# Layer 1's input projection with 27 pairs of channel tiles: seven products of halves in place of eight

## The chip, the core and the metric

One NeuronCore of a Trainium2 chip runs the whole kernel; the other cores are idle. The metric is device time in microseconds (us), the median of three runs. Engines are named as in the profile: PE is the matmul array (PEld its weight loads), DVE, ACT and POOL are the vector, scalar and GpSimd engines, SP is the queue that issues most of the loads.

## What is computed

Two layers over 512 tokens of width 1024. Layer 0 mixes pooling and a stick-breaking attention; layer 1 is a gated short convolution. The change is in layer 1, whose mixer is

```python
proj = h @ w_in                       # h: 512 x 1024, w_in: 1024 x 8192
gb, gc, u, gate = jnp.split(proj, [D_CONV, 2 * D_CONV, 3 * D_CONV], axis=-1)
u = gc * u
conv = conv_b + sum(up[:, j:j + s] * conv_w[j] for j in range(CONV_WIDTH))   # up: u, padded by 2
y = gb * conv * jax.nn.silu(gate)
return y @ w_out                      # 2048 x 1024
```

and h is the normalised input, scaled and shifted by parameters that come from a conditioning vector c (`ada`, a 1024 x 3072 matrix for each layer). All data is float32.

## The kernel before

Activations lie transposed in SBUF: 128 channels on the partitions, 512 tokens in a row. Each float32 operand of a matmul is split into two float32r parts, hi (the value rounded by a cast on ACT) and lo (the value minus hi, on DVE); `hilo` does both. A product is then three matmuls, hi·hi, hi·lo and lo·hi (`mm3`, lines 189 to 193), with float32 sums in PSUM.

A weight tile ("unit") is 128 x 1024: 128 output channels, eight blocks of 128 for the contraction. `load_upto` issues its 512 KB load on SP into `raw` (3 buffers), `split_upto` makes `whi` and `wlo` (3 buffers each), `next_unit` keeps a few units ahead of use. `mtile` multiplies one unit with h: 8 x 3 matmuls of 128 x 128 weights against 512 tokens.

Layer 1 (`layer1`, lines 819 to 892): the units of the first channel tile are multiplied in two halves of 256 tokens, while h is still being made for the second half. Then, for each of 16 channel tiles j, `mtile` runs four times in the order gc, u, gate, gb; DVE and ACT form gc·u, the convolution (`acc`), the gate's SiLU and the products, and split the result into `yh` and `yl`. After j = 7 and after j = 15 an output projection of 8 units follows (`outproj`, `outproj_norm`), each of which adds its result into x (`x_add`, line 226). Between the channel tiles `ada_next(1)` loads 512 KB of the conditioning matrix and takes a dot product on DVE (line 114), one after each j until the list `ada_rest` is empty; layer 0's first output projection does two per unit.

PE and SP run in the order in which the code is written. The order on DVE, ACT and POOL is set by a scheduler that works out priorities from the program; on the chip every engine takes its instructions strictly in that order and waits on semaphores for the others.

## Time and profile before

| | |
|---|---|
| median of three runs | 896.88 us (896.63 to 898.55) |
| profiled execution, its time | 897.1 us |
| profiled execution, its span | 895.4 us |
| PE busy, share of the span | 98% |
| DVE, ACT, POOL busy | 64%, 39%, 6% |
| granted clock of PE, mean | 0.992 of full speed |
| data moved | 106.69 MB, mean 119 GB/s |

The profile is of one execution. Its span, from the first to the last recorded instruction, is 1.7 us shorter than the time that is measured around it. Matmuls overlap in their records (a record of 0.39 us starts 0.23 us after the one before), so the busy share of PE says that PE always has something in hand; how fast it goes is read from the starts of its records.

### The profile page before, as it was taken

The numbers are of one execution on the slowest core, as the hardware profiler recorded it, in microseconds if no ns is written. First come the engines' busy times: TensorE is split into PE (matmuls) and PEld (weight loads), VectorE is DVE, ScalarE is ACT, GpSimd is POOL, SyncE is SP. The second block draws the span as 40 slices with busy tenths as digits, with TensorE's granted clock in tenths as the row PEclk, the third lists the DMA queues.
The fourth block names the chain that finished last, engine by engine and source line by source line (L and its number), as shares of the span: only waits on it lengthen the run. The fifth ranks groups of instructions, "written<-read, shape, count | busy, mean of one in ns | idle before, by whom it ended". The sixth has DMA issues, their size and how long they took to land.

```text
span 895.4 us, 10797 instructions
## 1 busy us (share of the span) xinstructions
PE 877.2 (98%) x4172; PEld 733.9 (82%) x4172; DVE 573.8 (64%) x816; ACT 353.5 (39%) x552; POOL 56.4 (6%) x106
## 2 busy tenths in 40 slices
PE   8999999999999999999999999999999999999995
PEld 5788788888888888888998888888888888888884
DVE  6989979788877777695665555445334444444445
ACT  5366564655312655564442222222122222222331
POOL 1002301202000102010000000000000000000002
PEclk9999999999999999999999999999999999999997
DMA  8852132123876221123413333333322233222202
GB/s 308 298 177 73 53 100 89 60 71 118 305 279 238 85 81 59 59 79 107 145 48 118 118 121 126 128 120 119 94 94 94 98 102 106 95 94 94 94 25 94
DMA packets 30725, 106.69 MB, mean 119 GB/s; under 512 B 3409, under 2 KB 3537, under 8 KB 30674
## 3 DMA queue, kind: packets, MB, share of 16 engines
q1 hardware_dynamic: 30386, 105.48, 34.7%
q8 instruction: 33, 0.54, 0.3%
q10 hardware_dynamic: 288, 0.52, 0.2%
q14 instruction: 18, 0.15, 0.1%
HBM read 103.90 MB, written 2.10 MB: 118 GB/s over the span
## 4 chain that ended last, share of the span: by engine, by line
PE 90%; DVE 6%; ACT 1%; issue 1%; DMA 1%; SPq 0%; POOL 0%; DVEq 0%; ACTq 0%
PE m L191 25%; PE m L192 25%; PE m L193 25%; PE zb L662 2%; PE av L397 2%; PE m L664 2%; PE z L384 1%; DVE f L368 1%; PE zb L143 1%; PE z L353 1%; PE zb L806 1%; PE zb L805 1%; PE zb L807 1%; PE z L354 1%; PE zb L191 1%
## 5 line engine op out<-in xcount | busy, mean ns | idle before, releaser
L60 ACT CAST whi<-raw 128x1024 fp32r<-128x1024 f32 (+1 forms) x137 | 142.5, 1041 | 411.7 <-PE m L192 323.9
L191 PE MATMUL m<-hh,whi 128*128 128x512 f32 x768 | 300.5, 391 | 0.6 <-DVE yt L408 0.6
L193 PE MATMUL m<-hh,wlo 128*128 128x512 f32 x768 | 299.1, 389 | 0.0
L192 PE MATMUL m<-hl,whi 128*128 128x512 f32 x768 | 299.0, 389 | 0.0
L61 DVE TENSOR_TENSOR wlo<-raw,whi 128x1024 fp32r<-128x1024 f32 (+1 forms) x137 | 165.1, 1206 | 114.2 <-ACT whi L60 110.8
L193 PEld LDWEIGHTS m<-hh,wlo 128*128 128x128 f32 x768 | 144.1, 188 | 30.2
L191 PEld LDWEIGHTS m<-hh,whi 128*128 128x128 f32 x768 | 144.2, 188 | 30.1 <-DVE yt L408 0.8
L192 PEld LDWEIGHTS m<-hl,whi 128*128 128x128 f32 x768 | 144.3, 188 | 29.2
L191 PE MATMUL m<-yh,whi 128*128 128x512 f32 (+1 forms) x288 | 105.7, 367 | 0.0
L192 PE MATMUL m<-yl,whi 128*128 128x512 f32 (+1 forms) x288 | 105.3, 365 | 0.0
L193 PE MATMUL m<-yh,wlo 128*128 128x512 f32 (+1 forms) x288 | 105.2, 365 | 0.0
L226 DVE SCALAR_TENSOR_TENSOR x<-m,small,x 128x512 f32<-128x512 f32 (+1 forms) x36 | 24.8, 691 | 64.1 <-PE m L193 64.1
L191 PEld LDWEIGHTS m<-yh,whi 128*128 128x128 f32 x288 | 54.3, 189 | 8.9
L192 PEld LDWEIGHTS m<-yl,whi 128*128 128x128 f32 x288 | 54.3, 189 | 8.8
L193 PEld LDWEIGHTS m<-yh,wlo 128*128 128x128 f32 x288 | 54.3, 189 | 8.8
L362 POOL TENSOR_SCALAR_AFFINE_SELECT s<-s 128x128 f32<-128x128 f32 x64 | 43.2, 698 | 270.2 <-ACT s L357 252.4
L368 DVE TENSOR_TENSOR_SCAN f<-f,mask 128x512 f32<-128x512 f32 (+1 forms) x64 | 52.2, 844 | 0.0
L846 DVE TENSOR_TENSOR u<-m,t 128x512 f32<-128x512 f32 x16 | 11.1, 692 | 56.0 <-PE m L193 49.6
L60 ACT CAST yh<-t 128x512 fp32r<-128x512 f32 x40 | 24.9, 621 | 45.7 <-DVE t L441 20.3
L859 DVE TENSOR_TENSOR t<-t,m 128x512 f32<-128x512 f32 x15 | 10.3, 688 | 50.3 <-PE m L193 50.3
L114 DVE CUSTOM_DVE_ANT_0 araw<-araw,cbc,cst 128x1024 f32<-128x1024 f32 x32 | 40.5, 1277 | 2.0 <-DMA araw<-in_ada 2.0
L845 POOL MEMSET u<- 128x16 f32 x16 | 1.8, 112 | 423.3 <-DVE t L854 347.5
(180 smaller groups left out, 972.1 us busy)
## 6 DMA issues: line engine op xcount, KB each, us to landing
raw<-in_w1m SPq DMA_DIRECT2D x64, 512.0 KB, 3.3
raw<-in_w0m SPq DMA_DIRECT2D x36, 512.0 KB, 3.3
araw<-in_ada SPq DMA_DIRECT2D x32, 512.0 KB, 4.9
ring<-in_ada SPq DMA_DIRECT2D x16, 512.0 KB, 5.7
raw<-in_w0o SPq DMA_DIRECT2D x16, 512.0 KB, 4.2
raw<-in_w1o SPq DMA_DIRECT2D x16, 512.0 KB, 3.2
raw<-in_w0s SPq DMA_DIRECT2D x8, 512.0 KB, 5.8
x<-in_x SPq DMA_DIRECT2D x8, 256.0 KB, 4.7
```

Source lines behind the costliest of these rows:

```text
L60: a = self.nc.scalar.copy(out=hi, in_=src)
L61: b = (eng or self.nc.vector).tensor_tensor(out=lo, in0=src, in1=hi.bitcast(F32), op=ALU.subtract)
L114: ins = nc.vector.tensor_tensor_reduce(raw, raw, self.cbc, 1.0, self.cst[:, b : b + 1], ALU.mult, ALU.add, col)
L191: mm(ps, wh, xh, start=first, stop=False)
L192: mm(ps, wh, xl, start=False, stop=False)
L193: mm(ps, wl, xh, start=False, stop=last)
L226: self.nc.vector.scalar_tensor_tensor(x, ps[:, sl], self.adacol(layer, 2, mt), x, ALU.mult, ALU.add)
L362: nc.gpsimd.affine_select(out=sw[:, d], in_=sw[:, d], pattern=[[-1, P]], compare_op=ALU.is_gt, fill=0.0, base=0, channel_multiplier=1,)
L368: nc.vector.tensor_tensor_scan(r, r, self.mask[:, S - n :][:, ::-1], 1.0, ALU.mult, ALU.max)
L397: self.nc.tensor.matmul(ps[:, kb * P :], vs[:, kb, c : c + P], t[:, o : o + w], start=(n == 0 and kb == 0), stop=(n == 1 and kb == 3),)
L662: mm(pv[bank], h[:, tok[bank]], w[:, :512], start=f and n == 0, stop=l and n == 2)
L664: mm(pq[bank - 4], w[:, col[bank - 4]], h, start=f and n == 0, stop=l and n == 2)
```

## The change

Channel tiles j = 2 to 15 of layer 1 are taken in pairs of weight tiles: (gc, u) of each j and (gb, gate) of each j but the last, 27 pairs. The contraction of 1024 is cut into two halves of 512 and the tokens into two halves of 256. Of a pair, W11 and W12 are the two halves of the first tile, W21 and W22 of the second; B11 to B22 are the quarters of h (first digit the half of the contraction, second the half of the tokens). In place of eight products of such halves seven are formed, of W11, W12, W22 and four sums of weights (S1 to S4) against B11, B21, B22 and four sums of quarters of h (T1 to T4). A product is 4 x 3 matmuls of 128 x 128 weights against 256 tokens (`product`). Tiles j = 0 and 1, the gate and gb of j = 15, and both output projections stay as they were.

T1 to T4 are made once (`make_t`, on DVE and ACT) during tile j = 1, from a float32 copy of h (`hf`, one more ACT instruction for each piece of h). The sums of weights are made per pair: `load_pair` loads the second tile into `r2`, the first into `r1`, half of the second once more into `r3` (all on SP), and then POOL issues a transfer that reads 512 KB from DRAM and adds it into `r2` (W11 and W21, so that `r2` holds W11 + W21 and W21 + W22); S2 and S4 are two further additions on DVE. `r1` takes the three `raw` buffers in turn, `r2` two buffers, `r3` two. `prep` splits each of the seven weights; the six buffers of `whi` and `wlo` hold the results, and splitting runs five products ahead of PE. `step` moves sums out of PSUM between the products: three results are read out from one bank as they accumulate. The last two products of a pair stand between those of the next pair.

All 24 dot products for layer 1's conditioning are now done in layer 0's first output projection (`ada_next(3)` in place of `ada_next(2)`); layer 1 has none. The first operation of the convolution moves from DVE to ACT.

```diff
...
@@ -69,14 +69,14 @@
         return len(self.units) - 1
     def load_upto(self, n):
-        while self.loaded < min(n, len(self.units)):
+        while self.loaded < min(n, self.limit):
...
-                    self.outproj(0, ys, lambda mt: self.ada_next(2))
+                    self.outproj(0, ys, lambda mt: self.ada_next(3))
...
+    PAIRED = range(2, 16)
...
     def plan_l1(self):
         io = self.io
         self.l1_first = len(self.units)
-        for g in range(2):
-            for j in range(8 * g, 8 * g + 8):
-                for part in (1, 2, 3, 0):
-                    self.add_unit(io["w1m"][part * 16 + j])
-            for mt in range(8):
-                self.add_unit(io["w1o"][mt, g])
+        self.limit = self.l1_first + 8
+        for j in range(2):
+            for part in (1, 2, 3, 0):
+                self.add_unit(io["w1m"][part * 16 + j])
+        for mt in range(8):
+            self.add_unit(io["w1o"][mt, 0])
+        for part in (3, 0):
+            self.add_unit(io["w1m"][part * 16 + 15])
+        for mt in range(8):
+            self.add_unit(io["w1o"][mt, 1])
...
+    def make_t(self):
+        nc = self.nc
+        ha, hb = slice(0, 256), slice(256, S)
+        sub = dict(op=ALU.subtract)
+        self.T = {}
+        t12 = self.ap.tile([P, 4, 1024], F32R, tag="vs", name="t12")
+        sums = []
+        for k in range(4):
+            f1, f2 = self.hf[k], self.hf[k + 4]
+            a = self.yp.tile([P, S], F32, tag="yl", name="ta")
+            b = self.yp.tile([P, S], F32, tag="yl", name="tb")
+            nc.vector.tensor_tensor(out=a[:, ha], in0=f1[:, ha], in1=f1[:, hb], **sub)
+            nc.vector.scalar_tensor_tensor(a[:, hb], f2[:, hb], -1.0, a[:, ha], ALU.mult, ALU.subtract)
+            nc.vector.tensor_tensor(out=b[:, ha], in0=f2[:, hb], in1=f1[:, hb], **sub)
+            nc.vector.scalar_tensor_tensor(b[:, hb], a[:, hb], -1.0, f2[:, ha], ALU.mult, ALU.subtract)
+            sums.append((a, b))
+        for k in range(4):
+            a, b = sums[k]
+            d = t12[:, k]
+            self.hilo(d[:, :S], d[:, S:], a)
+            e = self.ap.tile([P, 1024], F32R, tag="sf"[k % 2], name="t34", bufs=2)
+            self.hilo(e[:, :S], e[:, S:], b)
+            for n, (t, o) in enumerate(((d, 0), (d, 256), (e, 0), (e, 256))):
+                self.T[n + 1, k] = (t[:, o : o + 256], t[:, S + o : S + o + 256])
...
+    def load_pair(self, m1, m2):
+        nc, w = self.nc, self.io["w1m"]
+        i = self.pair_no = getattr(self, "pair_no", -1) + 1
+        r1 = self.wp.tile([P, 1024], F32, tag="raw", name="r1", bufs=3)
+        r2 = self.ap.tile([P, 1280], F32, tag=("ah", "al")[i % 2], name="r2")[:, :1024]
+        r3 = self.ap.tile([P, S], F32, tag=("kle", "klo")[i % 2], name="r3")
+        nc.sync.dma_start(r2, w[m2])
+        nc.sync.dma_start(r1, w[m1])
+        nc.sync.dma_start(r3, w[m2, :, 512:])
+        nc.gpsimd.dma_start(
+            r2.rearrange("p (a c) -> p a c", a=2),
+            w[m1 : m2 + 1 : m2 - m1, :, :512].rearrange("a p c -> p a c"), accum_op=ALU.add,
+        )
+        return dict(r1=r1, r2=r2, r3=r3)
...
+    def prep(self, pr, what):
+        nc = self.nc
+        r1, r2 = pr["r1"], pr["r2"]
+        k1, k2 = slice(0, 512), slice(512, 1024)
+        src = {
+            "W11": r1[:, k1], "W12": r1[:, k2], "W22": pr["r3"], "S1": r2[:, k2], "S2": r2[:, k2],
+            "S3": r2[:, k1], "S4": r1[:, k2],
+        }[what]
+        if what == "S2":
+            nc.vector.tensor_tensor(out=src, in0=src, in1=r1[:, k1], op=ALU.add)
+        self.prod_no += 1
+        d = self.wp.tile([P, 1024], F32R, tag=("whi", "wlo")[self.prod_no % 2], name="wp", bufs=3)
+        self.hilo(d[:, k1], d[:, k2], src)
+        if what == "W12":
+            nc.vector.tensor_tensor(out=src, in0=src, in1=r2[:, k2], op=ALU.add)
+        pr[what + "d"] = d
...
+    def product(self, pr, what, mov, bank, first):
+        d = pr.pop(what + "d")
+        mm = self.nc.tensor.matmul
+        ps = pr[bank]
+        for k in range(4):
+            hi, lo = d[:, k * P : (k + 1) * P], d[:, 512 + k * P : 512 + (k + 1) * P]
+            bh, bl = self.moving(mov, k)
+            mm(ps, hi, bh, start=first and k == 0, stop=False, skip_group_check=True)
+            mm(ps, hi, bl, start=False, stop=False, skip_group_check=True)
+            mm(ps, lo, bh, start=False, stop=k == 3, skip_group_check=True)
...
+    def step(self, pr, n):
+        nc = self.nc
+        ha, hb = slice(0, 256), slice(256, S)
+        copy = nc.scalar.copy
+        if n == 1:
+            pr["X"] = self.zbank()[:, ha]
+            self.product(pr, "W11", "B11", "X", True)
+            pr["t12"] = self.t512("sgp")
+            copy(out=pr["t12"][:, ha], in_=pr["X"])
+        elif n == 5:
+            pr["Z"] = self.zbank()[:, ha]
+            self.product(pr, "S1", "T1", "Z", True)
+        elif n == 6:
+            self.product(pr, "S2", "T2", "X", False)
+            copy(out=pr["t12"][:, hb], in_=pr["X"])
+        elif n == 2:
+            pr["Y"] = self.mbank()[:, ha]
+            self.product(pr, "W12", "B21", "Y", True)
+            pr["o1"] = self.t512(pr["tag"])
+            nc.vector.tensor_tensor(out=pr["o1"][:, ha], in0=pr["Y"], in1=pr["t12"][:, ha], op=ALU.add)
+        elif n == 7:
+            self.product(pr, "S3", "T3", "X", False)
+            t3 = self.t512("u%d" % pr["odd"], S + PAD, 1)[:, ha]
+            copy(out=t3, in_=pr["X"])
+            pr["o2"] = self.t512(pr["tag"])
+            nc.vector.scalar_tensor_tensor(pr["o2"][:, hb], pr["Z"], -1.0, t3, ALU.mult, ALU.subtract)
+        elif n == 4:
+            self.product(pr, "W22", "T4", "X", False)
+            nc.scalar.activation(pr["o2"][:, ha], pr["X"], AF.Copy, scale=-1.0)
+        else:
+            self.product(pr, "S4", "B22", "Z", False)
+            nc.vector.tensor_tensor(out=pr["o1"][:, hb], in0=pr["Z"], in1=pr["t12"][:, hb], op=ALU.add)
+            pr["done"](pr["o1"], pr["o2"])
...
+        nc.scalar.activation(
+            acc, cu[:, PAD:], AF.Identity, scale=wc(2), bias=self.cst[:, C_CB + j : C_CB + j + 1]
+        )
...
+        hf = [self.ap.tile([P, 2, S], F32, tag="sf"[i % 2], name="hf", bufs=2) for i in range(4)]
+        self.hf = [hf[k // 2][:, k % 2] for k in range(KT)]
...
-                self.make_h(1, k, ra, sl)
+                t = self.h_scale(1, k, ra, sl)
+                self.h_hi(1, k, t, sl)
+                self.h_lo(1, k, t, sl)
+                nc.scalar.activation(self.hf[k][:, sl], t, AF.Identity, bias=self.adacol(1, 0, k))
...
+        pairs = []
+        for j in self.PAIRED:
+            pairs.append(dict(m=(16 + j, 32 + j), tag="t", done=done_a(j), odd=0, j=j))
+            if j < 15:
+                pairs.append(dict(m=(j, 48 + j), tag="sga", done=done_b(j), odd=1, j=j))
+        order = []
+        for i, pr in enumerate(pairs):
+            last = pairs[i - 1] if i else None
+            order += [(pr, 1), (pr, 5)]
+            if last and not last.get("early"):
+                order += [(last, 4)]
+            order += [(pr, 6), (pr, 2)]
+            if last and not last.get("early"):
+                order += [(last, 3)]
+            order += [(pr, 7)]
+            if pr["j"] == 8 and pr["odd"]:
+                pr["early"] = True
+                order += [("out", 0), (pr, 4), (pr, 3)] + [("out", mt) for mt in range(1, 8)]
+        order += [("tail", 0), (pairs[-1], 4), (pairs[-1], 3)]
+        loaded = [0]
+        def load_to(n):
+            while loaded[0] < min(n, len(pairs)):
+                pr = pairs[loaded[0]]
+                pr.update(self.load_pair(*pr["m"]))
+                loaded[0] += 1
...
+        classic(1, self.mtile, sums=lambda: (self.make_t(), load_to(1)))
+        load_to(2)
+        prepped = 0
+        hold = [1 + next(i for i, pr in enumerate(pairs) if pr["j"] == 8 and pr["odd"])]
+        for i, (pr, n) in enumerate(order):
+            while prepped < min(len(order), i + 6):
+                q, m = order[prepped]
+                if not isinstance(q, str):
+                    if m == 1:
+                        load_to(min(pairs.index(q) + 2, hold[0]))
+                    if "r1" not in q:
+                        break
+                    self.prep(q, self.WEIGHT[m])
+                prepped += 1
+            if pr == "out":
+                if n == 0:
+                    self.limit += 8
+                if n == 6:
+                    hold[0] = len(pairs)
+                    load_to(loaded[0] + 1)
+                w = self.next_unit(1)
+                ps = self.mbank()
+                self.out_mm(ps, w, [ys[q] for q in range(8)], range(8))
+                self.x_add(1, n, ps)
+            elif pr == "tail":
+                self.limit = len(self.units)
+            else:
+                self.step(pr, n)
+        sg = classic(15, self.mtile, accs.pop(15))
+        ys = [ys[q] for q in range(8, 16)]
...
```

How this stands on the engines. DVE in the middle of layer 1, before: one channel tile. `wlo` are splits of weights, `u`, `t_` and `m` belong to the convolution and the gating, `araw` is a dot product of the conditioning.

```order
L61 TENSOR_TENSOR yl<-t_4612,yh 128x512
L114 ISA araw,small<-araw,cbc,cst 128x1024
L114 ISA small 128x1
L124 TENSOR_SCALAR small<-small 128x1
L61 TENSOR_TENSOR wlo<-raw,whi 128x1024
L846 TENSOR_TENSOR u<-m,t 128x512
L849 TENSOR_SCALAR t_4757<-u,cst 128x512
L61 TENSOR_TENSOR wlo<-raw,whi 128x1024
L854 SCALAR_TENSOR_TENSOR t_4757<-u,cst,t_4757 128x512 x2
L61 TENSOR_TENSOR wlo<-raw,whi 128x1024
L859 TENSOR_TENSOR t_4757<-t_4757,m 128x512
L860 TENSOR_TENSOR t_4757<-t_4757,sga 128x512
```

DVE at the same place after: `wp` are splits of weights of one pair (`r_4771`, `r_4772`) and of the pair before it (`r_4638`), lines 891 and 896 the additions for S2 and S4, lines 930, 936 and 942 the reads out of PSUM.

```order
L61 TENSOR_TENSOR wp<-r_4771,wp 128x512
L61 TENSOR_TENSOR wp<-r_4772,wp 128x512
L891 TENSOR_TENSOR r_4772<-r_4772,r_4771 128x512
L61 TENSOR_TENSOR wp<-r_4638,wp 128x512
L930 TENSOR_TENSOR sga<-m,sgp 128x256
L61 TENSOR_TENSOR wp<-r_4772,wp 128x512
L942 TENSOR_TENSOR t<-zb,sgp 128x256
L952 TENSOR_TENSOR u<-t 128x512
L61 TENSOR_TENSOR wp<-r_4771,wp 128x512
L896 TENSOR_TENSOR r_4771<-r_4771,r_4772 128x512
L960 SCALAR_TENSOR_TENSOR t_4983<-u,cst,t_4983 128x512
L936 SCALAR_TENSOR_TENSOR sga<-zb,u_5003 128x256
```

Two pairs (four weight tiles, one channel tile) take 30 rows on DVE after, where one channel tile took 12 or 13 before, four of them twice as wide.

POOL from the end of layer 0 on, before: 16 small fills (the zeros ahead of the convolution) and nothing else until the final scaling.

```order
L429 MEMSET u 128x16
L362 AFFINE_SELECT s<-s 128x128 x8
L845 MEMSET u 128x16 x16
L888 TENSOR_TENSOR o<-x_81,u 128x256
L888 TENSOR_TENSOR o<-x_82,u 128x256
```

POOL in the middle of layer 1 after: the transfers that add into `r2` (here called by their buffer numbers), one per pair, and the fills.

```order
L951 MEMSET u 128x16
L875 DMA r_4772<-in_w1m 128x2x512
L875 DMA r_4907<-in_w1m 128x2x512
L951 MEMSET u 128x16
L875 DMA r_5042<-in_w1m 128x2x512
L875 DMA r_5177<-in_w1m 128x2x512
```

Each of these 27 transfers waits on POOL for the plain load of the same `r2` on SP, and that load for the last split that reads the `r2` of two pairs before (S3, the last weight of a pair to be split from it).

DVE in layer 0's first output projection, as the difference: a third dot product per unit, ahead of the split of the next unit and of the next addition into x.

```order
 L114 ISA araw,small<-araw,cbc,cst 128x1024
 L114 ISA small 128x1
+L114 ISA araw,small<-araw,cbc,cst 128x1024
+L114 ISA small 128x1
 L61 TENSOR_TENSOR wlo<-raw,whi 128x1024
 L226 SCALAR_TENSOR_TENSOR x_79<-m,small,x_79 128x512
```

The same piece comes back for each of the 8 units; the loads of the conditioning matrix on SP are three per unit there, too.

## Rows read from the trace of the kernel before

**Rows 1.** The page: busy time of the engines, and the chain by engine.

```profile
PE 877.2 (98%) x4172; PEld 733.9 (82%) x4172; DVE 573.8 (64%) x816; ACT 353.5 (39%) x552; POOL 56.4 (6%) x106
...
PE 90%; DVE 6%; ACT 1%; issue 1%; DMA 1%; SPq 0%; POOL 0%; DVEq 0%; ACTq 0%
```

**Rows 2.** Windows: length, busy PE, PEld, DVE, ACT, POOL, clock, DMA share, GB/s.

```profile
466.70:640.30 173.60, 173.60 (x772) 143.91 (x772) 87.95 (x115) 47.87 (x57) 0.90 (x8) 1.00 0.35 116
...
683.80:857.90 174.10, 174.10 (x770) 144.16 (x769) 75.73 (x89) 49.32 (x60) 0.67 (x6) 1.00 0.29 96
```

**Rows 3.** PE's timeline in layer 1, 512 tokens: start, duration; 15 rows left out.

```profile
682.63 0.39 PE L191 MATMUL m<-hh,whi 128*128 128x512 f32 x1
...
686.26 0.39 PE L192 MATMUL m<-hl,whi 128*128 128x512 f32 x1
```

**Rows 4.** PE's timeline at tile j = 0, 256 tokens; 39 rows left out.

```profile
462.81 0.28 PE L192 MATMUL zb<-hl,whi 128*128 128x256 f32 x1
...
467.61 0.28 PE L193 MATMUL zb<-hh,vw 128*128 128x256 f32 x1
467.73 0.40 PE L191 MATMUL m<-hh,whi 128*128 128x512 f32 x1
```

**Rows 5.** DVE and ACT by shape: count, busy us, mean ns, idle before.

```profile
L61 DVE TENSOR_TENSOR yl<-t,yh 128x512 fp32r<-128x512 f32 x40 | 27.2, 685 | 1.4 <-ACT yh L60 1.4
L854 DVE SCALAR_TENSOR_TENSOR t<-u,cst,t 128x512 f32<-128x512 f32 x32 | 23.9, 748 | 0.6
L416 DVE TENSOR_TENSOR vs<-zb,vs 128x256 fp32r<-128x256 f32 x8 | 3.3, 416 | 0.0
...
L60 ACT CAST yh<-t 128x512 fp32r<-128x512 f32 x40 | 24.9, 621 | 45.7 <-DVE t L441 20.3 <-DVE t L860 12.9 <-DVE t L718 8.4
L415 ACT CAST vs<-zb 128x256 fp32r<-128x256 f32 x8 | 3.2, 398 | 0.0
```

**Rows 6.** DVE's timeline where it works without a pause, three places.

```profile
238.98 0.41 DVE L419 TENSOR_TENSOR vs<-zb,vs 128x256 fp32r<-128x256 f32 x1
239.31 0.41 DVE L416 TENSOR_TENSOR vs<-zb,vs 128x256 fp32r<-128x256 f32 x1
...
319.17 0.68 DVE L718 TENSOR_TENSOR t<-yt,sga 128x512 f32<-128x512 f32 x1
319.77 1.22 DVE L61 TENSOR_TENSOR wlo<-raw,whi 128x1024 fp32r<-128x1024 f32 x1
320.90 0.69 DVE L61 TENSOR_TENSOR yl<-t,yh 128x512 fp32r<-128x512 f32 x1
...
444.63 0.87 DVE L178 SCALAR_TENSOR_TENSOR hl<-t,small,hh 128x256 fp32r<-128x256 f32 x2
```

**Rows 7.** Loads, issue to landing: line 75 in 500:800, then line 107 anywhere.

```profile
DMA to landing us min/median/max: 3.1/3.3/5.3
...
DMA to landing us min/median/max: 3.2/5.1/7.9
```

**Rows 8.** DVE's timeline behind tile j = 0; five rows left out.

```profile
467.47 0.69 DVE L846 TENSOR_TENSOR u<-m,t 128x512 f32<-128x512 f32 x1 [6.42 <-ACT t L842]
...
473.60 0.69 DVE L61 TENSOR_TENSOR yl<-t,yh 128x512 fp32r<-128x512 f32 x1 [0.69 <-ACT yh L60]
```

**Rows 9.** Layer 0's first output projection: windows, then DVE's timeline.

```profile
230.00:236.00 6.00, 6.00 (x29) 4.95 (x28) 5.14 (x9) 1.26 (x2) 0.00 (x0) 1.00 0.99 391
257.00:263.00 6.00, 6.00 (x28) 4.95 (x28) 4.85 (x9) 1.06 (x1) 0.00 (x0) 1.00 0.83 291
...
277.20 0.75 DVE L226 SCALAR_TENSOR_TENSOR x<-m,small,x 128x512 f32<-128x512 f32 x1 [0.88 <-PE m L193]
...
288.93 1.23 DVE L61 TENSOR_TENSOR wlo<-raw,whi 128x1024 fp32r<-128x1024 f32 x1 [1.73 <-PE z L384]
```

**Rows 10.** PEld's timeline with 256 tokens: weight loads.

```profile
443.18 0.19 PEld L191 LDWEIGHTS m<-yh,whi 128*128 128x128 f32 x1
443.30 0.19 PEld L192 LDWEIGHTS m<-yl,whi 128*128 128x128 f32 x1
```

78 lines of the change are left out of this document (49 added, 29 removed).

## The prediction

> **What bounds the kernel now.** I read the page first: PE is busy 98% of the span and is 90% of the chain of work that ended last, while DVE is at 64% and ACT at 39% [rows 1]. Then the windows of layer 1: on both sides of its first output projection PE is busy without a gap at full clock, DVE for half of the time, ACT for less than a third, the DMA engines at 0.29 to 0.35 [rows 2]. So layer 1 lasts as long as PE's list of matmuls, and what counts is the distance between the starts of two of them. With 512 tokens 16 matmuls take 3.63 us, 0.2268 us each [rows 3]. With 256 tokens, which this kernel already has at tile j = 0, 40 matmuls take 4.80 us, 0.120 us each [rows 4]. Half the tokens cost 53% of the time, not 50%; eight products of halves for eight would lose, seven for eight can win.
>
> **PE.** A pair of tiles takes 2 x 24 matmuls of 512 now: 48 x 0.2268 = 10.89 us. Seven products of 12 matmuls of 256 take 84 x 0.120 = 10.08 us. 27 pairs save 27 x 0.81 = **21.8 us**, if PE never waits. The matmuls keep their shapes of weights and their order hi·hi, hi·lo, lo·hi, so I see no other change of pace.
>
> The Trainium skill, TensorE: Matmul & The Clock Gate, Back-to-back issue gap, speaks against this: it gives a sustained spacing of about 81 ns for 128 columns and 131 ns for 512. By a straight line between them (an estimate from that page) 256 columns take 98 ns, a pair would go from 6.3 to 8.2 us, and the kernel would lose 52 us. The trace disagrees at both widths, 0.227 us at 512 and 0.120 at 256, so the rule gets no chance below.
>
> **DVE in the steady state** is the nearest other engine. Two pairs are 30 rows of DVE: 22 two-operand instructions of 512 (14 splits, 4 additions of weights, 4 for the convolution and the gating), 2 steps of the convolution, 4 + 2 reads of 256 out of PSUM. Their durations are 685, 748, 416 ns [rows 5] and 0.48 us for the last kind, 19.2 us in all. But back to back they start sooner than they end: 0.60 us apart at 512, 0.33 at 256, and two of the last kind take 0.87 us together [rows 6]. That makes 22 x 0.60 + 2 x 0.75 + 4 x 0.33 + 2 x 0.40 = 16.8 us against PE's 20.16 for the same two pairs. DVE goes from half busy to 83%, off the path. ACT: 17 instructions of 512 at about 621 ns and 8 copies of 256 at 398 [rows 5], 13.8 us of 20.16. Splits run five products ahead, 7.2 us, so a late DVE does not reach PE at once. Each read out of PSUM has two products (2.9 us) before PE needs the bank again; it takes 0.4 us on ACT or DVE. Both at nothing; what it costs if the cover goes is the second rival.
>
> **The transfers.** Loads grow from 1 MB per pair to 1.25 MB on SP and 0.5 MB that POOL adds into `r2`: 1.84 million bytes in 10.08 us, 182 GB/s. The trace has moved 391 GB/s over 6 us [rows 9], so there is room. What the trace does not have is a transfer issued by POOL that adds. Its latency matters through one loop, because `r2` has two buffers: S3 of a pair is split, the plain load of `r2` two pairs on starts, then the addition, then that pair's S1 can be split, and its S3 after 13 more rows of DVE. In steps: S1's cast and subtraction 1.2 us; the 13 rows 7.4 us (at the starts above); the plain load 3.3 us [rows 7]; four hand-overs at 0.1, an estimate, 0.4. Together 12.3 us; the loop has two pairs' time, 20.16 us. So the addition is **free up to 7.9 us**. Its bounds: 3.1 us, a quiet plain load, and 15.8 us, twice the longest load when the queue was full [rows 7]. I take 6.6, two median loads, since the quiet ones are nearest (182 GB/s is not a full queue) and it has two streams to read. That is under 7.9, so the cost is nothing.
>
> On that price the Trainium skill has two sentences. Collectives: The Full Stack, The bandwidth ceiling, says an add in the DMA engine is slow because it reads two sources, not because of the addition; DMA: Bandwidth & Descriptors, Anatomy of one DMA, gives 2.0 us plus bytes at 436 GB/s for a transfer issued by GpSimd. With the bytes counted twice that is an estimate of 4.4 us, and the sum would be the same. No row here shows either.
>
> **Where the pairs begin.** DVE is empty until 467.5 and done with tile j = 0 at 474.2 [rows 8]. Then follow, by DVE's order: 16 quarter sums for T1 to T4 (5.8 us), a split of a unit (1.1), the convolution of j = 1 (2.1), 8 splits of T (4.8), the first three splits and two additions of weights (3.0), one gating step (0.6) and S2's split (0.6): 492.2. PE has tile j = 1 from 467.73 [rows 4] for 4 x 24 x 0.2268 = 21.8 us, to 489.5, and wants S2 two products later, at 492.4. That leaves 0.2 us, too little to call free: +1.0 us, between 0 and 4 (a further 3 us of waits on ACT, which has the same splits to feed). The extra copy of h on ACT runs at 0.4 us beside PE's 1.44 per piece: nothing.
>
> **Layer 0's first output projection** gets a third dot product per unit. DVE idles 0.88 us of each 5.44 now [rows 9]; a dot and its small step take 1.3. It falls behind by 0.4 a unit, some 3 us over 8, and has 1.73 us of idle behind the stage [rows 9]. The loads, four of 512 KB in 5.44 us, are 385 GB/s, just what the trace has once reached. PE has two units split ahead, 10.9 us: +0.5, between 0 and 4. The 8 dots that leave layer 1 were off the path: 0.
>
> **Middle and end.** Around the output projection after j = 8 the buffers of weights change hands; a split of 1024 (2.3 us) must fit into the two products that PE still has (2.9 us). It fits: +0.4 for both places, between 0 and 2. Output projections and final scaling are unchanged.
>
> **Sum.** 897.1 (the profiled execution; its span is 1.7 less) - 21.8 + 1.0 + 0.5 + 0.4 = 877.2; the median of the runs lies 0.2 lower, so **877.0 us**. With all small terms at their ends 875.1 to 885; I call 874 to 882 the forecast's own range.
>
> **Rival 1, the slower one: the addition closes the loop.** If POOL's transfer takes longer than 7.9 us, every two pairs last that much longer, 13.5 times. At 9.35 us the whole net gain of 19.9 is gone; beyond that the kernel is slower than before: 10.2 us (two median busy loads) gives 877 + 31 = 908, 15.8 gives 984. For it: nothing in the trace bounds it from above, it has two streams, and POOL has to be woken in between. Against: loads in layer 1 land in 3.3 us. 33%, of which 21 above the break-even.
>
> **Rival 2: DVE becomes the bound.** If the rows run at full duration because each waits for the one before or for ACT, two pairs take 19.2 us, and with 0.15 us for each of 14 waits for a cast (an estimate; the one wait of this kind behind j = 0 is 0.69, most of it the cast [rows 8]) 21.3: 13.5 x 1.14 = 15 us, 892. For it: DVE's order mixes splits with reads that wait for PE. Against: the overlap of rows is there at all three places, and five products of lead absorb single waits. 10%.
>
> **Rival 3: narrow matmuls wait for their weights.** A weight load lasts 0.19 us, longer than the 0.120 between matmuls, and is hidden only because two overlap [rows 10]. With none hidden a pair would take 84 x 0.19 = 16.0 us, the kernel 897 + 27 x 5.1 = 1035. At tile j = 0 nothing of it is seen: 1%.
>
> That the change does less than it says is no rival: the built order of PE has 2268 matmuls of 256 in place of 1296 of 512.
>
> **The numbers.** Forecast 56%, rival 1 33%, rival 2 10%, rival 3 1%. Faster by over 0.2% (1.8 us, about what a measurement can tell from no change): 56 + 10 of rival 1 + 6 of rival 2 = 72%. Within 0.2%: 3%. Slower: 21 + 3 + 1 = 25%. The range goes from 874 to 908: it leaves out some 3% below, and above it the part of rival 1 beyond 10.2 us and rival 3, some 15%.
>
> **What would show it.** Starts of matmuls in a product 0.120 us apart, seven products in 10.1 us, PE without gaps in layer 1, and its windows 7% shorter for the same channel tiles: the first term. DVE near 83% of those windows, and rows 0.60 us apart: rival 2 out. The landing of POOL's transfers under 7.9 us, and no wait of ACT's cast of S1 on DMA that ends a PE gap: rival 1 out; if it is right, PE has one gap per pair, just ahead of the product with S1, and the waits name that transfer. PE's gap at the first pair, between 489 and 493 us, shows the 1.0. The forecast is wrong if PE shows a gap in every pair, whoever causes it.

## The result, and the profile after

The changed kernel takes **887.6 us** (median of 4 runs, 885.6 to 889.3) against 897.7 for the kernel before: ratio 0.9885, interval 0.9858 to 0.9912. A second set of four runs, beside later experiments, gave 885.1 and 0.9863 (0.9847 to 0.9879). It is faster and inside the range, but the gain is 10.1 us (11.9 in the second set) where the forecast of 877.0 promised 19.9.

The page of the changed kernel, the lines that answer to [rows 1], then the group and the transfer that the pairs hang on (columns: busy us, mean ns, idle before and its releasers; KB, us to landing):

```profile
PE 861.1 (97%) x5144; PEld 765.7 (87%) x5144; DVE 689.4 (78%) x1094; ACT 452.8 (51%) x821; POOL 89.3 (10%) x133
...
PE 81%; DVE 11%; DMA 4%; ACT 2%; issue 2%; DVEq 0%; SPq 0%; POOL 0%; ACTq 0%; POOLq 0%
...
L60 ACT CAST wp<-r 128x512 fp32r<-128x512 f32 x189 | 113.7, 621 | 71.7 <-DMA r<-in_w1m 32.7
...
r<-in_w1m POOLq DMA_DIRECT2D x27, 512.0 KB, 6.8
```

PE's share of the chain fell from 90 to 81%: DVE and DMA now hold part of the end. The windows inside the pairs, beside [rows 2] (length, busy PE, PEld, DVE, ACT, POOL, clock, DMA share, GB/s), show that this is not the steady state: PE has no gap, DVE 85 to 88%.

```profile
540.00:560.00 20.00, 20.00 (x169) 20.00 (x168) 17.60 (x32) 12.54 (x26) 2.54 (x3) 1.00 0.73 189
...
720.00:740.00 20.00, 20.00 (x169) 20.00 (x168) 16.91 (x30) 12.10 (x25) 2.69 (x4) 1.00 0.71 184
```

PE's timeline there (start, duration; 173 rows left out) has 174 matmuls of 256 in 20.88 us, 0.120 each, as in [rows 4]:

```profile
569.03 0.28 PE L906 MATMUL zb<-t,wp 128*128 128x256 f32 x1
...
589.91 0.28 PE L906 MATMUL zb<-t,wp 128*128 128x256 f32 x1
```

So I laid the two PE timelines side by side, by the same matmul in both. **Stretch B** runs from the last matmul of layer 0's first output projection to the first matmul of 256 tokens behind it, which stands in layer 0's second output projection (before: 282.21 to 431.30; after: 283.82 to 438.13), **stretch L** from there to the last row of matmuls (885.21; 873.46). The change makes B 5.2 us longer, 149.09 to 154.31, and L 18.6 shorter, 453.91 to 435.33. Ahead of B the profile after is 1.6 us late, behind L 0.3; 18.6 - 5.2 - 1.6 - 0.3 = 11.5, the distance of the two profiled executions (897.1 and 885.6). The 1.6 are not the change: the stretch from the first matmul to B took between 280.2 and 283.2 us in the profiles of this study, and kernels with two and with three dots per unit lie mixed in that range.

B's loss has one place. PE after, then before, at the first attention behind the output projection:

```profile
296.06 0.74 PE L397 MATMUL av<-ah,vs 128*128 128x512 f32 x4
300.07 1.68 PE L397 MATMUL av<-al,vs 128*128 128x512 f32 x4 [3.27 <-DVE small L124]
301.54 2.29 PE L384 MATMUL z<-ident,s 128*128 128x128 f32 x10
303.55 0.51 PE L191 MATMUL m<-hh,whi 128*128 128x512 f32 x1
```

```profile
294.46 0.74 PE L397 MATMUL av<-ah,vs 128*128 128x512 f32 x4
295.03 0.81 PE L397 MATMUL av<-al,vs 128*128 128x512 f32 x4
295.68 1.27 PE L384 MATMUL z<-ident,s 128*128 128x128 f32 x10
296.71 0.48 PE L191 MATMUL m<-hh,whi 128*128 128x512 f32 x1
```

From start to start the first step is 4.01 us in place of 0.57, a wait of 3.44 for `al` (the row names a `small` step of a dot, which ended on DVE just behind the first `al`). The four matmuls behind it then take 1.47 in place of 0.65 and the ten transposes 2.01 in place of 1.03, together 1.8 more: after the idle stretch the clock is at its lower level, 1.2 GHz, for most of 3.5 us (granted 0.53):

```profile
300.00:303.50 3.50, 3.43 (x14) 2.92 (x15) 3.50 (x8) 3.09 (x5) 0.00 (x0) 0.53 0.17 34
```

DVE after shows what `al` waited for: two of the last dots, then `al`; below it `al` in the kernel before (three in one row):

```profile
295.90 1.28 DVE L114 CUSTOM_DVE_ANT_0 araw<-araw,cbc,cst 128x1024 f32<-128x1024 f32 x1
...
298.01 1.27 DVE L114 CUSTOM_DVE_ANT_0 araw<-araw,cbc,cst 128x1024 f32<-128x1024 f32 x1
...
299.32 0.69 DVE L61 TENSOR_TENSOR al<-z,ah 128x512 fp32r<-128x512 f32 x1
```

```profile
291.61 1.62 DVE L61 TENSOR_TENSOR al<-z,ah 128x512 fp32r<-128x512 f32 x3
```

With the 1.6 of the start taken off, `al` is 6.1 us late. Before, the first of the three is done at 292.30 and PE takes it at 295.03, so 2.7 us of that are covered and 3.4 reach PE.

### The profile page after: what moved, and what is told of

The parts are those of the page before. It is cut to its first block, busy times and chain, and to the rows that moved or that the text cites. A ratio compares the mean times of both kernels' runs of the same rounds, so it can differ in the third digit from the quotient of the medians.

```text
span 883.9 us, 13503 instructions
## 1 busy us (share of the span) xinstructions
PE 861.1 (97%) x5144; PEld 765.7 (87%) x5144; DVE 689.4 (78%) x1094; ACT 452.8 (51%) x821; POOL 89.3 (10%) x133
## 4 chain that ended last, share of the span: by engine, by line
PE 81%; DVE 11%; DMA 4%; ACT 2%; issue 2%; DVEq 0%; SPq 0%; POOL 0%; ACTq 0%; POOLq 0%
PE m L191 12%; PE m L192 12%; PE m L193 12%; PE zb L906 8%; PE zb L908 8%; PE zb L907 8%; PE zb L662 2%; DVE araw L114 2%; PE av L397 2%; PE m L664 2%; PE z L384 1%; DVE f L368 1%; PE m L908 1%; PE m L907 1%; PE m L906 1%
## 5 line engine op out<-in xcount | busy, mean ns | idle before, releaser
L61 DVE TENSOR_TENSOR wp<-r,wp 128x512 fp32r<-128x512 f32 x189 | 124.6, 684 | 39.0 <-ACT wp L60 38.7
L60 ACT CAST wp<-r 128x512 fp32r<-128x512 f32 x189 | 113.7, 621 | 71.7 <-DMA r<-in_w1m 32.7
L191 PE MATMUL m<-hh,whi 128*128 128x512 f32 x336 | 132.5, 394 | 0.6 <-DVE yt L408 0.6
L193 PE MATMUL m<-hh,wlo 128*128 128x512 f32 x336 | 131.0, 390 | 0.0
L192 PE MATMUL m<-hl,whi 128*128 128x512 f32 x336 | 131.0, 390 | 0.0
L906 PE MATMUL zb<-t,wp 128*128 128x256 f32 x432 | 122.6, 284 | 1.7 <-ACT u L934 0.9
L908 PE MATMUL zb<-t,wp 128*128 128x256 f32 x432 | 122.4, 283 | 0.0
L907 PE MATMUL zb<-t,wp 128*128 128x256 f32 x432 | 122.2, 283 | 0.0
L906 PEld LDWEIGHTS zb<-t,wp 128*128 128x128 f32 x432 | 82.9, 192 | 2.5 <-ACT u L934 1.3
L908 PEld LDWEIGHTS zb<-t,wp 128*128 128x128 f32 x432 | 82.9, 192 | 0.2 <-DVE wp L61 0.2
L907 PEld LDWEIGHTS zb<-t,wp 128*128 128x128 f32 x432 | 82.9, 192 | 0.0
L193 PEld LDWEIGHTS m<-hh,wlo 128*128 128x128 f32 x336 | 63.1, 188 | 13.4
L191 PEld LDWEIGHTS m<-hh,whi 128*128 128x128 f32 x336 | 63.2, 188 | 13.1 <-DVE yt L408 0.8
L192 PEld LDWEIGHTS m<-hl,whi 128*128 128x128 f32 x336 | 63.2, 188 | 12.3
```

Of the source, the lines that this page charges most:

```text
L60: a = self.nc.scalar.copy(out=hi, in_=src)
L61: b = (eng or self.nc.vector).tensor_tensor(out=lo, in0=src, in1=hi.bitcast(F32), op=ALU.subtract)
L191: mm(ps, wh, xh, start=first, stop=False)
L192: mm(ps, wh, xl, start=False, stop=False)
L193: mm(ps, wl, xh, start=False, stop=last)
L906: mm(ps, hi, bh, start=first and k == 0, stop=False, skip_group_check=True)
```

## Experiments: the five microseconds in layer 0

**The kernel before with this one part of the change.**

```diff
-                    self.outproj(0, ys, lambda mt: self.ada_next(2))
+                    self.outproj(0, ys, lambda mt: self.ada_next(3))
```

> The kernel before with this one part of the change alone: three dots per unit in layer 0's first output projection, none in layer 1. All of the result is computed. If the 5.25 us come from this part and from nothing else: PE's gap of about 4 us at the first attention behind the stage, time about 902.9 against 897.7, and layer 1 as long as before. If they come from the whole of the change (another place of the buffers, the start-up): 897.7.

Measured 903.7 us, ratio 1.0065 (1.0049 to 1.0082). L is 453.90, as before; B is 156.28, 7.2 longer, some 6 of them at the same place (PE's timeline):

```profile
295.91 0.74 PE L397 MATMUL av<-ah,vs 128*128 128x512 f32 x4
300.67 1.68 PE L397 MATMUL av<-al,vs 128*128 128x512 f32 x4 [4.02 <-DVE small L124]
```

The third dot per unit alone makes the loss, and nothing else of the change does.

**The third dot without its load.** The added function is called in place of `ada_next(3)`.

```diff
+    def ada_third(self):
+        self.ada_next(1)
+        a = self.ada_rest.pop(0)
+        raw = self.ada_load(*a)
+        self.ada_dot(*a, raw, True)
+        self.ada_dot(*self.ada_rest.pop(0), raw, True)
```

> The changed kernel, but in layer 0's first output projection the third dot of each unit has no load of its own: it runs over the tile of the second dot (eight conditioning columns of layer 1 get other values). DVE keeps all 24 dots there, the queue loses 8 of its 32 loads of 512 KB. Theory A (the stage is held by its loads: 4 x 512 KB per unit took 6.93 us in the changed kernel's trace, PE needs 5.44): PE's gap behind the stage (4.0 us from the matmul ahead, with 1.8 us of half clock behind it) is gone or under 1 us, time about 883. Rival B (DVE holds it: three dots, an addition and a split need some 5.8 us of 5.44): the gap stays near 4 us, time 887 to 888.

**Its load without the dot.**

```diff
+    def ada_third(self):
+        self.ada_next(2)
+        a = self.ada_rest.pop(0)
+        raw = self.ada_load(*a)
+        ins = self.nc.vector.tensor_scalar_add(self.adacol(*a), raw[:, 0:1], 1.0)
+        self.tc.keep_in_program_order(ins)
```

> The changed kernel, but the third dot of each unit in layer 0's first output projection is replaced by an addition of 1 to one column of the tile that was loaded for it (eight conditioning columns of layer 1 get other values). The load stays, DVE loses 8 dots of 1.3 us. Theory A (the loads hold the stage): PE's gap behind the stage stays at 3 to 4 us, the loads of weights there stay near 7 us from issue to landing, time 886 to 888. Rival B (DVE holds it): the gap is gone, time 882 to 883.

Measured 880.9 and 883.9 us; B is 149.08 and 150.32. **Both theories fell**: with the load taken away all of the loss goes, with the dot taken away 4.0 of 5.2. DVE's timelines, the last dot and the first `al` behind it, without the load and then without the dot:

```profile
290.07 1.27 DVE L114 CUSTOM_DVE_ANT_0 araw<-araw,cbc,cst 128x1024 f32<-128x1024 f32 x1
...
293.99 1.62 DVE L61 TENSOR_TENSOR al<-z,ah 128x512 fp32r<-128x512 f32 x3
```

```profile
292.25 1.28 DVE L114 CUSTOM_DVE_ANT_0 araw<-araw,cbc,cst 128x1024 f32<-128x1024 f32 x1
...
294.54 1.62 DVE L61 TENSOR_TENSOR al<-z,ah 128x512 fp32r<-128x512 f32 x3
```

Measured from the start of B, the first `al` is 0.7 us later than in the kernel before without the load and 3.4 later without the dot; against the lead of 2.7 that leaves PE nothing to wait for in the first and 0.6 in the second (PE's gap there: 0.54).

The units' additions to x are 5.61 us apart (mean of seven) with the dots alone, 5.88 with the loads alone, 5.99 with both, against PE's 5.44. With both, the last three dots run into the attention. They are coupled: a dot frees one of three buffers, SP stands at the next load until it is free, and the next unit's weights are queued behind it. SP's queue in the changed kernel, and the landing of the weights' loads (line 75, from 244 to 300 us) there and in the kernel before:

```profile
281.24 3.72 SPq L107 DMA_DIRECT2D araw<-in_ada  x3
285.05 0.38 SPq L75 DMA_DIRECT2D raw<-in_w0m  x1
288.17 3.72 SPq L107 DMA_DIRECT2D araw<-in_ada  x3
291.98 19.78 SPq L75 DMA_DIRECT2D raw<-in_w0m  x6
```

```profile
DMA to landing us min/median/max: 6.4/7.0/7.3
```

```profile
DMA to landing us min/median/max: 3.2/4.3/5.5
```

ACT's casts waited 16.1 us, four times, for the weights' loads issued from 240 to 300 us, and never for those of the kernel before; DVE waited in turn for the casts. The additions of the last two units are 6.93 us apart there. How much of it is SP's order and how much the fuller queue (301 GB/s from 248 to 290 us against 273) these runs don't separate.

## Experiments: the loop over r2

In the changed kernel the cast of S1 waits for POOL's adding transfer in 23 of 27 pairs. One pair in the steady state: the plain load of `r2` (SP), the adding transfer (POOL), the cast of S1 (ACT), the split of S3 (second of three rows, DVE), and SP's load of the same buffer two pairs on:

```profile
570.83 0.33 SPq L872 DMA_DIRECT2D r<-in_w1m  x1
...
590.88 0.33 SPq L872 DMA_DIRECT2D r<-in_w1m  x1
```

```profile
575.51 1.22 POOL L875 DMA_DIRECT2D r<-in_w1m  x1 [8.66 <-DVE sga L930]
```

```profile
582.25 0.62 ACT L60 CAST wp<-r 128x512 fp32r<-128x512 f32 x1 [1.11 <-DMA r<-in_w1m]
```

```profile
589.57 1.89 DVE L61 TENSOR_TENSOR wp<-r,wp 128x512 fp32r<-128x512 f32 x3
```

4.7 + 6.7 + 8.6 = 20.05 us, and PE needs 20.16 for two pairs: the loop is closed, without slack. (The 4.7 are 4.0 for the landing, the median of the 27 plain loads, and 0.7 until POOL issues.) PE is still served because splits run ahead: S1's cast starts 5.3 us (median) ahead of its product where 6.7 is the most; at 3.9 PE waits. It did so at the third pair (513 and 518 us): ACT stood 3.5 us at S1's cast, and the copies out of PSUM, for which PE waited, were queued behind it.

**Three buffers for r2**, run twice.

```diff
-        r2 = self.ap.tile([P, 1280], F32, tag=("ah", "al")[i % 2], name="r2")[:, :1024]
+        r2 = self.wp.tile([P, 1024], F32, tag="araw", name="r2", bufs=3)
```

> The changed kernel with three buffers for r2 in place of two (in the three tiles that the conditioning loads leave free in layer 1); nothing else. All of the result is computed. In the changed kernel the cast of S1 waits for POOL's adding transfer in 23 of 27 pairs and starts 5.3 us (median) ahead of its product; where it starts 3.9 us ahead, PE waits. Theory: the loop over r2's two buffers is all but closed, and is what leaves no slack; with three the cast starts 6 us or more ahead, ACT's 33 us of waits on these transfers fall under 5, and the PE gaps at the third pair (0.8 and 0.6 us at 513 and 518 us) go: 886.5 against 887.6. Rival: the transfers themselves are what is late (the queue, or POOL): waits and gaps as they are, 887.6.

> The changed kernel with three buffers for r2 once more. 883.3 in the median; in the profile no PE gap over 0.5 us between the second pair and the last, PE's gap behind layer 0's first output projection as in the changed kernel.

> The changed kernel itself once more, on the chip and in the rounds of these runs. If two buffers cost what the medians say: 3.5 to 4.5 us above the run with three, so 887 to 888, with a gap of several us in one or two pairs that the first profile did not show. If they cost what the first profile shows: 1 to 2 us above it.

Measured 883.3, then 883.6 beside 885.1 for the change itself. L is 433.09 with three buffers (the second run's profile), 435.33 and 435.01 with two: **1.9 to 2.2 us**, and the gaps at the third pair are gone. The adding transfer is no faster (median 7.3 us), yet S1's cast has its full 6.7 us of lead in every pair, and ACT's waits on it are gone: its group now reads

```profile
L60 ACT CAST wp<-r 128x512 fp32r<-128x512 f32 x189 | 116.7, 620 | 67.8 <-PE zb L908 19.9
```

So it is not a slow transfer that costs, but a loop in which the transfer has no room. The edit has a side effect: the three tiles are others, and the first load of a pair goes out about 10 us sooner. A run further down that keeps the old two tiles and adds one (886.0 us, dots elsewhere) has the same full lead up to the middle, so the third buffer does it there. The 4 us between the first medians were more than the loop; the second pair of medians and the profiles agree on 1.6 to 2.2.

**A plain transfer in place of the adding one** (the diff takes `accum_op=ALU.add` away).

> The changed kernel with POOL's transfer as a plain one of the same bytes and the same places (nothing is added, so the output has other values). It measures what adding costs a transfer: 6.8 us (median) from issue to landing with the addition. If the second stream that is read makes it (two plain loads of 3.3 are 6.6): about 3.5 to 4 without it, S1's cast then has its full lead of 6.7 us. If it is the queue of POOL: 6 to 7 again. Time between 886.5 and 887.6 either way, since the gaps that it can take away are about 1 us in all.

Measured 884.2 us, L 433.08, as with three buffers: a transfer that is 2.1 us shorter opens the loop as well. (The time is below what was expected, since the loop is worth 2 us and not 1.) The transfers' line without the addition, then with it:

```profile
L875 POOL DMA_DIRECT2D r<-in_w1m x27: 722/722/869, 480.7 to 789.3; - x27
...
DMA to landing us min/median/max: 4.2/4.7/6.3
```

```profile
L875 POOL DMA_DIRECT2D r<-in_w1m x27: 1210/1217/1332, 479.0 to 791.0; - x27
...
DMA to landing us min/median/max: 6.2/6.8/9.6
```

Adding costs 2.1 us of landing and 0.5 us of POOL's time for 512 KB. The Trainium skill, Collectives: The Full Stack, The bandwidth ceiling, puts the price of an addition on the second source read and makes it a factor of two; the trace agrees with a price, but 6.8 to 4.7, for one transfer until it lands and not for the throughput of a ring as there, is a factor of 1.45.

**A second, small adding transfer behind it**, with two buffers and with three.

```diff
+        nc.gpsimd.dma_start(
+            r2.rearrange("p (a c) -> p a c", a=2)[:, :, :16],
+            w[m1 : m2 + 1 : m2 - m1, :, :16].rearrange("a p c -> p a c"), accum_op=ALU.add,
+        )
```

> The changed kernel, with a second, small adding transfer behind POOL's: 16 columns of either half of r2 are added once more, so S1, S2, S3 and S4 (and the output) get other values. It waits for the first one's landing and so lengthens only the latency T from the first issue to r2's last byte, at next to no bytes: by 3 to 5 us, to some 10 to 12. By the loop over r2's two buffers (free up to T = 7.9, then 13.5 times the excess): 10 gives 916, 12 gives 943, with one PE gap ahead of a product with S1 or behind it in every pair or two. Rival: splits run five products ahead, so 4 us more disappear in that lead, 888 to 890.

> The run with a second, small adding transfer behind POOL's (945.3 us; output of other values), now with three buffers for r2. Theory: what cost 57.7 us was the loop over two buffers; with three it has three pairs' time, 30.2 us, against some 12.3 + 10.2, and all of it goes: about 884, S1's cast 6 us or more ahead of its product. Rival: POOL's transfer is late by itself, since POOL waits for the plain load and then twice for its own: 930 or more.

Measured 945.3 and 914.9 us. The small transfer is issued 7.1 us behind the first and lands in 3.2 (medians); S1 has its data 11.0 us behind the first issue, 4.2 later than before. With the loop as it measures (13.3 us and the transfer, not 12.3) two pairs last 4.1 us longer, 13.5 x 4.1 = 55 us. The profile with two buffers (949.6 us) has 43 us of idle time in 25 gaps of the pairs (1.7 in 4 in the changed kernel), and L is 64.8 us longer: the rest is matmuls more than 0.120 us apart behind the longer gaps, at the lower clock. One gap (PE's timeline), and the window around it (clock 0.91):

```profile
568.10 0.39 PE L910 MATMUL zb<-t,wp 128*128 128x256 f32 x1 [3.54 <-ACT sgp L929]
```

```profile
560.00:620.00 60.00, 51.88 (x393) 51.27 (x393) 39.38 (x69) 28.26 (x58) 12.43 (x12) 0.91 0.60 148
```

The third buffer gives back 30 of the 57.7 us, not all: each theory holds half. What stays is POOL's own sequence, with three buffers:

```profile
743.73 1.22 POOL L875 DMA_DIRECT2D r<-in_w1m  x1 [2.48 <-issue]
...
751.77 1.22 POOL L879 DMA_DIRECT2D r<-in_w1m  x1 [6.69 <-DMA r<-in_w1m]
755.68 1.22 POOL L875 DMA_DIRECT2D r<-in_w1m  x1 [2.70 <-issue]
```

One pair's two transfers take POOL 11.95 us of a pair's 10.08; the next pair's does not start before the small one has landed. Two pairs of it, 23.9 us, are nearly as long as the loop of 24.3, so with two buffers the one can't be told from the other.

## Experiments: where the eight dots can stand

All of these have two dots per unit in layer 0's first output projection, and B is 149.0 to 149.1 in each. L tells what the eight dots cost elsewhere.

**Beside the first eight pairs**, each dot with its load; then with the loads two pairs ahead (`ada_ahead` issues the next load, `ada_do` computes the oldest loaded dot).

```diff
                 self.step(pr, n)
+                if n == 2:
+                    self.ada_next(1)
```

```diff
...
+        self.ada_ahead()
+        self.ada_ahead()
         prepped = 0
...
                 self.step(pr, n)
+                if n == 2:
+                    self.ada_ahead()
+                    self.ada_do()
```

> The changed kernel with two dots per unit in layer 0's first output projection, as before, and the remaining eight in layer 1, one behind the second product of W12 kind of each of the first eight pairs. All of the result is computed. Theory A and rival B agree that the 5.25 us behind the first output projection come back: time about 882.3, the stage behind it at the offset of the stage ahead. What it tells: whether layer 1 has room for them. DVE is at 84 to 88% of the pairs' windows; one dot adds 1.3 us to 10.08 us of a pair, 97 to 100% if nothing overlaps. If layer 1 has room, its 2268 matmuls of 256 keep their 275 us; if DVE is then the bound, they take up to 8 us more and the gain is lost.

> As the run with eight dots beside layer 1's first pairs, but each dot's load is issued two pairs ahead of it and ahead of the next pair's loads have to be. All of the result is computed. Theory C (there DVE lost its time by standing in order behind a load of 512 KB that SP issued too late; 3.6 us of such waits are in its trace; DVE itself has room): time about 882 to 884, DVE near 94% in these pairs, no wait of a dot on its load. Rival D (DVE is full at 84 to 88%, since the rest are hand-overs): 1.3 us of every one of the eight pairs comes back as PE gaps, 890 to 893. Rival E (the loads on SP delay the plain loads of r2, and with them POOL's adding transfer): the cast of S1 starts 3.9 us ahead of its product in most of these pairs, the point at which PE begins to wait, time 885 to 890.

Measured 893.0 (L 447.76) and 890.1 (L 445.85). In the first, DVE stood in order at a dot whose load was late; in the second no dot waits, yet PE does, and DVE is busy 16.2 to 18.3 of 20 us, hardly more than without the dots (one of four windows):

```profile
563.35 1.28 DVE L114 CUSTOM_DVE_ANT_0 araw<-araw,cbc,cst 128x1024 f32<-128x1024 f32 x1 [3.60 <-DMA araw<-in_ada]
```

```profile
540.00:560.00 20.00, 18.81 (x155) 18.41 (x154) 16.85 (x33) 10.33 (x23) 2.54 (x3) 1.00 0.77 211
```

The time lies where rival D had put it, but DVE is not full there. S1's cast of the third to ninth pair starts 3.9 to 4.4 us ahead, about the point of waiting, as rival E said, but not for its reason: the plain loads of r2 are on time (4.7 us to POOL's issue, as without the dots). The loop is longer in two other places: the adding transfer takes 7.9 to 8.2 us from its issue to S1's cast in five of these pairs in place of 6.7, and from S1's cast to the plain load two pairs on it is 9.8 to 10.0 us in place of 8.6 to 8.9, one dot (1.28) more in DVE's order. The loop without slack pays for every load on SP and every row of DVE.

**Beside the middle output projection**, with two buffers for r2; with a third one from the dots' tiles; with three of its own and the dots in other tiles; and this with T3 and T4 split later. The first's diff, and what the other three add, in this order:

```diff
...
             if pr == "out":
+                self.ada_do()
...
                 self.x_add(1, n, ps)
+                self.ada_ahead()
...
                 self.step(pr, n)
+                if n == 2 and pairs.index(pr) in (10, 11, 12):
+                    self.ada_ahead()
```

```diff
+        if i % 3 == 2:
+            r2 = self.wp.tile([P, 1024], F32, tag="araw", name="r2", bufs=3)
...
```

```diff
...
+        r2 = self.wp.tile([P, 1024], F32, tag="araw", name="r2", bufs=3)
...
+            tag = ("ah", "al")[len(self.ada_rest) % 2]
+            raw = self.ap.tile([P, 1280], F32, tag=tag, name="araw")[:, :1024]
...
+                if pairs.index(pr) == 13 and n in (2, 7):
+                    self.ada_ahead()
```

```diff
...
+            if i == 0:
+                self.make_t34()
```

> The changed kernel with two dots per unit in layer 0's first output projection; the other eight run beside the output projection in the middle of layer 1, one ahead of each unit's addition to x, their loads issued at least three units earlier. All of the result is computed. DVE is busy 16.6 of 38 us there and the engines of the DMA half, so eight dots (11.6 us of DVE) and 4 MB of loads fit beside 43.5 us of PE. If the 5.25 us behind layer 0's first output projection come only from the third dot and its load: they are gone and layer 1 is as long as in the changed kernel, 882.3 against 887.6. If layer 1 loses again as it did with the dots beside its pairs (10 us): 890 or more.

> Eight dots beside layer 1's middle output projection, as above, together with a third buffer for r2 (every third pair uses a tile of the conditioning loads). All of the result is computed. If both mend what they are meant to: 882.3 less 1 us, about 881.3, with S1's cast 6 us ahead of its product. If the dots or the third buffer are worth nothing: 882.3 or 886.5.

> Three buffers for r2 in the tiles of the conditioning loads, as in the run that gave 883.3, and layer 1's last eight dots beside its middle output projection, in two tiles of layer 0's attention that are free there, their first two loads issued only when the loads for pairs are held. All of the result is computed. The 5.25 us behind layer 0's first output projection are gone, the cast of S1 starts 6.7 us ahead of its product in every pair, no PE gap between the first pair's beginning and the last product: 883.3 less 5 gives 878.5; if the 4 us that the third buffer alone has gained were partly chance, 881.

> The one above, and T3 and T4 (8 of the 16 rows of splitting the quarter sums, 4 on ACT and 4 on DVE) are split behind the first six weights of the first pair in place of ahead of them. All of the result is computed. The gap of 2 us that PE has in the first product of the first pair, waiting for DVE's split, shrinks by up to 2: 876.5 to 878.5. If DVE is then late for T3, the seventh product, the gap moves there and the time stays.

Measured 883.2, 886.0, 884.3 and 883.1 us; L 440.44, 441.35, 439.35 and 438.78. That is at or little below the change itself: all lose in L most or all of what they gain in B. In the first, two loads for dots were issued beside one pair's adding transfer, which then took 11.3 us, and PE had a gap of 3.7:

```profile
609.11 0.91 SPq L107 DMA_DIRECT2D araw<-in_ada  x2
```

```profile
620.12 0.62 ACT L60 CAST wp<-r 128x512 fp32r<-128x512 f32 x1 [6.11 <-DMA r<-in_w1m]
```

In the others the first pair behind the middle got its loads late, since SP stood at a dot's load: S1's cast starts 0.7 us ahead of its product. The gap that splitting T3 and T4 later was to close, 2 us at the first pair, was not there in the run without it either (four other profiles have it, with 1.8 to 2.6 us); what that edit is worth stays open.

**Two repairs of that**: dots and loads earlier; the pair's loads ahead of the last dot's.

```diff
-                if pairs.index(pr) == 13 and n in (2, 7):
+                if pairs.index(pr) in (12, 13) and n in (2, 7):
+                    if len(self.ada_loaded) > 1:
+                        self.ada_do()
                     self.ada_ahead()
```

```diff
-                if n == 6:
+                if n == 5:
                     hold[0] = len(pairs)
                     load_to(loaded[0] + 1)
```

> Three buffers for r2, T3 and T4 split later, two dots per unit in layer 0's first output projection; the other eight beside the last pair ahead of layer 1's middle output projection (two) and beside that projection (six), so that their last load is out of SP's queue before the loads for the pairs behind it. All of the result is computed. In the run that had all eight beside the projection the pair behind it got its adding transfer 10 us late (S1's cast 0.7 us ahead of its product) and PE had gaps of 2.2, 1.1 and 1.0 us there, with half clock behind each. If those go: about 883.1 less 5, 878. If they stay, since three pairs' loads still go out at once there: 883.

> The run with three buffers for r2, eight dots beside layer 1's middle output projection and T3 and T4 split later (883.1 us), with one line changed: the loads of the first pair behind the middle are released one unit earlier, and so stand in SP's queue ahead of the last dot's load, which waits there for a dot. All of the result is computed. If that wait (5.8 us on SP) is what made the adding transfer of that pair late: PE's gaps of 2.2, 1.1 and 1.0 us behind the middle go, with the half clock behind them, and the time is 878 to 879. If the burst of loads of three pairs makes it late: S1's cast of that pair stays under 4 us ahead of its product, and the time at 882 to 883.

Measured 889.0 and 888.3 us. Both fell: each moved the wait. In the first SP had the loads for dots ahead of the output projection's weights (26 us in one row, PE idle for 9.9); in the second ACT had S1's cast, waiting 8.8 us for a transfer, ahead of the cast of the last unit's weights:

```profile
605.26 26.48 SPq L136 DMA_DIRECT2D araw<-in_ada  x4
```

```profile
673.02 1.14 ACT L60 CAST wp<-r 128x512 fp32r<-128x512 f32 x2 [8.84 <-DMA r<-in_w1m]
...
676.18 1.04 ACT L60 CAST whi<-raw 128x1024 fp32r<-128x1024 f32 x1
```

**One dot beside every second pair, three buffers for r2**, T3 and T4 split later, and the eighth dot beside the middle output projection. The part of the diff that is new:

```diff
-                    self.outproj(0, ys, lambda mt: self.ada_next(3))
+                    self.outproj(0, ys, lambda mt: self.ada_next(2))
...
+                q = pairs.index(pr)
+                if n == 2 and q < 14 and (q == 0 or q % 2):
+                    self.ada_ahead()
+                    if q:
+                        self.ada_do()
...
```

> Three buffers for r2, T3 and T4 split later, two dots per unit in layer 0's first output projection; of the other eight, seven stand beside every second pair of layer 1's first half, each with its load two pairs ahead, the last one beside the third unit of the middle output projection. All of the result is computed. DVE goes from 86% to some 92% of those pairs, S1's cast keeps 6 us of lead with three buffers. If the two causes (5.3 to 7 us in layer 0, 1 to 3 us of the loop over r2) are what lay between the change and its forecast: 878 to 879. If DVE or the shared queue has no room for one more dot in two pairs: gaps of about 1 us in the first half's pairs, 882 to 885.

Measured **877.6 us** (876.0 to 878.3, 5 runs), ratio 0.9766 (0.9752 to 0.9781): it beats both kernels. B is 149.07, L 433.27, S1's cast has 6.7 us of lead in every pair, PE has no gap in the first half though DVE is at 93%:

```profile
540.00:560.00 20.00, 20.00 (x169) 20.00 (x168) 18.59 (x33) 12.46 (x25) 2.56 (x3) 1.00 0.72 203
```

Stretches B and L together are 582.3 us, 589.6 in the changed kernel; the forecast's terms make 583.1 of the 603.0 before. So the two causes account for the difference: 4.7 us of it in B, 1.8 in L, as the changed kernel was profiled. That the median also comes within 0.6 us of the forecast is partly luck: two sets of runs of the changed kernel differ by 2.4. And no run has the dots beside every second pair with two buffers, or beside every pair with three, so what made the room, the third buffer or the distance between the dots, is not separated.

## Why the prediction was half right

The step that failed is the price of layer 0's first output projection, put at 0.5 us and measured at 5.2. A second, smaller miss is the loop over r2, priced at nothing, where it cost 2.

- **PE, 27 x 0.81 = 21.8 us: right.** 0.120 us per matmul of 256 in 2268 matmuls. L is 20.8 us shorter where almost nothing waits (433.1), so only 1.0 stood against it there, 0.6 of it the gap at the last pair that every version has. The weight loads are hidden at this pace: rival 3 is out.
- **DVE: right.** 83% forecast, 85 to 88 measured, and 93 without a gap in the last run. Rival 2 is out: a busy share near full does not bound PE here while splits run ahead.
- **The adding transfer, 6.6 us: right (6.8). The loop around it: wrong by 1.0 us.** I had 12.3 us for the rest of the loop and so "free up to 7.9"; it is 13.3, and free up to 6.9, with 6.7 to 6.8 used. From S1's cast to the end of S3's split it takes the 8.6 us that I had summed; the part that was wrong is the plain load with its hand-overs, 3.7 from the rows of a quieter stage [rows 7], 4.7 here (4.0 to land, 0.7 until POOL issues). So rival 1 was not out: it ran at its edge and cost 2 us, most of it at the third pair, and a second transfer on POOL, 4.2 us more of latency, cost 57.7, of which a third buffer gave back 30. The mechanism was in the text; a third of the chance on it was not too much. The sign that I had named was off: PE waits not for S1 but for a copy out of PSUM that stands behind S1's cast on ACT.
- **Where the pairs begin, +1.0, and middle and end, +0.4: right in size.** By the starts of matmuls in the changed kernel 0.8 us at the first pair and 0.8 at the last; the 1.3 at the third pair belong to the loop. The wait at the first pair is gone, too, in the run with three buffers, so whether DVE's rows made it, as I had it, is open.
- **Layer 0's first output projection, +0.5: the term that was mis-sized**, 5.2 us (5.0 to 8.2 in other profiles of the same part, and the profiled execution of the changed kernel was the fastest of both its sets, so 5.2 is at the low end). I had seen that DVE falls behind and that the loads are at the queue's limit, and took them one by one: 0.4 us a unit for the one, room enough for the other. Together, in one order on SP and one on DVE, they made 0.55 a unit and 1.5 in the last. And I named the wrong cover: two units of split weights hide a late DVE from the projection, which indeed has no gap. But behind it stands an attention whose `al` has only 2.7 us of lead, behind the 1.73 us of idle that I had counted [rows 9]; DVE reached it 6.1 us late. The dots alone made it 0.7 late, which the forecast would have covered. On top came 1.8 us at the lower clock, which no term had.
